# Sums of the last layer's weights by adding DMAs: begun at the first output projection in place of the first attention, at a shorter interval

## The chip, the core and the metric

The kernel runs on one core of a Trainium2 chip. The metric is the device time of one execution in microseconds, the median of several runs. Five engines work beside each other, each through its own instructions in a fixed order: PE (TensorE, matrix products), ACT (ScalarE), DVE (VectorE), POOL (GpSimd) and SP (SyncE, which here only issues DMAs). ACT and POOL issue DMAs too, as instructions among their others.

## The reference

A two-layer encoder over 512 tokens (a grid of 8 x 64) of width 1024, in float32:

```python
for layer in range(2):
    hn = rmsnorm(h, norm_mix[layer])
    if layer == 0:   # 8 heads of grouped-query attention and 8 of latent attention, one output projection
        h = h + hybrid_attention(hn, ...)
    else:            # 16 heads, each query sees a clamped 8 x 16 window, learned bias
        h = h + neighbourhood_attention(hn, ...)
    h = h + sq_relu_mlp(rmsnorm(h, norm_ffn[layer]), ffn_w_up[layer], ffn_w_down[layer])
return rmsnorm(h, final_norm)

def sq_relu_mlp(h, w_up, w_down):
    u = jax.nn.relu(h @ w_up)
    return (u * u) @ w_down      # 1024 -> 4096 -> 1024
```

## The kernel before

Everything lies feature by token: `hT` holds the residual as 8 tiles of 128 features x 512 tokens. For float32 accuracy each operand is split into a high part (ACT rounds it, `whi`) and a low part (DVE or POOL subtracts, `wlo`), and a product is three matmuls, high x high, high x low and low x high (lines 515 to 517). Weights come by DMA from the SP queue into `raw` or a slot `a`, ACT and DVE split them (lines 212 and 202), PE uses them; the loads run up to five chunks ahead.

Most of the two MLPs uses seven products in place of eight (Strassen's scheme). The weights of such a product are sums of blocks. In `seven_chunk` POOL makes the sums in three instructions (lines 302 to 304) out of a loaded chunk, then ACT (line 308) and DVE (line 309) split the result, then PE runs 21 matmuls of 256 columns (lines 388 to 390).

The down product of the last layer's MLP is done in another way, in three sweeps over 11 pairs of row blocks. Its sums are made ahead, in DRAM, by `SumsAhead`: for each of the 11 pairs, ACT issues two copies of 512 KB from the weight tensor into a DRAM buffer `made` (line 810), and POOL issues four DMAs of 256 KB that add one half of a row block to another (line 804): two that add from the weight tensor and, one and two pairs later, two that add `made` to `made`. That is 22 copies and 44 additions. They are pinned to their places in the program (`keep_in_program_order`); who reads the sums is the sweep near the end (line 1304).

What paces them is a beat. `tick(us)` is called with each three matmuls and each quarter of an attention head, with a nominal time; whenever `every` nominal microseconds have gone by, one step of the generator `steps()` is taken, which issues one copy or one addition. `drain()` ahead of the sweeps takes what is left.

The stages in the order of the program: the first input projection; the first attention (`attend`: 16 heads of 4 query blocks, with the second part of the input projection, the latent projections and a part of the output projection filled in between the heads' matmuls); the rest of the output projection; the first MLP (`mlp(0)`: products with 6, 8 and 8 hidden blocks of plain or seven-fold form, then 10 more); the second attention (`attend_C`, whose order on PE, ACT, DVE and POOL is written out by hand); its output projection; the last MLP. Outside the second attention a scheduler orders each engine's instructions by its own estimates, so instructions near an added or removed one can change places.

In an attention head of the first kind PE makes scores (line 1039), DVE takes the row minimum (line 1043, in place of a maximum because the sign is turned) and a reciprocal (line 1046), ACT the exponential (line 1045), POOL the division (line 1047); PE transposes (line 1014), ACT and DVE split (lines 1016 and 1017), PE multiplies with the values (line 1027). Queries of the second to fourth pair of heads get their rotary positions in `rope_q` and `sum_q`: eight small DMAs from SP swap partitions (line 572), POOL multiplies (lines 576 and 577), DVE adds (line 645), ACT and DVE split (lines 647 and 648), and three more DMAs from SP place the parts (lines 649 to 651).

Of the kernel before, what the change touches and what calls it, by code (L numbers as in the profile page):

```python
# [30 lines left out]
def f32(ap):  # L31
    return ap.bitcast(F32)
# [3 lines left out]
def encoder_kernel(ctx: ExitStack, tc: tile.TileContext, ins, out, dbg=None):  # L36
# [24 lines left out]
    def nm(s):  # L61
        cnt[0] += 1
        return f"{s}_{cnt[0]}"
# [18 lines left out]
    def sbk():  # L82
        return bank("s", 2)

    def stb():
        return bank("t", 2)

    def ob():
        return bank("o", 1)
# [4 lines left out]
    def tiny(n, dt=F32):  # L94
        return tp.tile([P, n], dt, tag=f"ti{n}", name=nm("ti"))
# [369 lines left out]
    def tiles(c0, n):  # L465
        return [(c0 + o, min(P, n - o)) for o in range(0, n, P)]
# [5 lines left out]
    class Fill:  # L472
# [8 lines left out]
        def step(self):  # L481
            try:
                self.credit -= next(self.q[0][1])
            except StopIteration:
                self.q.pop(0)
# [15 lines left out]
    beat = dict(left=0.0, every=1.0, work=iter(()))  # L501

    def tick(us):
        beat["left"] -= us
        if beat["left"] <= 0:
            beat["left"] += beat["every"]
            next(beat["work"], None)
# [285 lines left out]
    class SumsAhead:  # L793
# [11 lines left out]

        def steps(self):
            for kp in range(self.n + 3):
                if kp < self.n:
                    for z in range(2):
                        tc.keep_in_program_order(ACT.dma_start(self.made[kp, z], self.w[kp, z]))  # L810
                        yield
                for back, to, src, of in ((1, (1, 1), (0, 1), self.w), (1, (0, 1), (0, 0), self.w),
                                          (2, (0, 0), (1, 1), None), (3, (1, 0), (0, 0), None)):
                    if 0 <= kp - back < self.n:
                        self.add(kp - back, to, src, of)
                        yield
# [166 lines left out]
    def fold(o, e):  # L983

        if e == 0:
            hold["pair"] = scratch()
        a, c, pair = 64 * e, scratch(), hold["pair"]
        ACT.activation(c[0:64, :], o[64:128, :], AF.Copy)

        def add():  # L990
            DVE.tensor_tensor(pair[a : a + 64, :], o[0:64, :], c[0:64, :], op=ALU.add)
            if e:
                O.append(Slot())
                soon_a(lambda o=O[-1]: split(pair, o.pair()))

        soon(add)
# [6 lines left out]
    def attend(heads, step):  # L1003


        late_t, late_v = [], []

        def transpose(h, i, p):
            if i % 2 == 0:
                h["pt"] = Slot(), Slot()  # L1010
            h3, l3 = (s_.t.rearrange("p (k q) -> p k q", k=4)[:, :, (i % 2) * P : (i % 2 + 1) * P] for s_ in h["pt"])
            tb = stb()
            for k in range(4):
                PE.transpose(tb[:, k * P : (k + 1) * P], p[:, k * P : (k + 1) * P], ident)
            t3 = tb.rearrange("p (k q) -> p k q", k=4)
            ACT.activation(h3, t3, AF.Copy)
            DVE.tensor_tensor(l3, t3, f32(h3), op=ALU.subtract)
            if i % 2:
                late_v.append((h, i // 2, h["pt"]))

        def values(h, half, pt):
            if half == 0:
                h["o"] = ob()
            o = h["o"]
            for k in range(4):
                for n, m in enumerate(pt):
                    PE.matmul(o[:, 256 * half : 256 * half + 256], h["vlhs"](k), m.t[:, 256 * k : 256 * k + 256],
                              start=k == 0 and n == 0, stop=k == 3 and n == 1, skip_group_check=True)
            for s_ in pt:
                s_.free()  # L1030
            if half:
                fold(o, h["e"])
                h["after"]()

        def scores(h, i):
            s = sbk()
            pl = h["passes"](i)
            for n, (lh, rh) in enumerate(pl):
                PE.matmul(s, lh, rh, start=n == 0, stop=n == len(pl) - 1)  # L1039
            h["done"](i)  # L1040
            t = tiny(4)
            p = pp.tile([P, 512], F32, tag="p", name=nm("p"))
            DVE.tensor_tensor_reduce(p, s, zeros.to_broadcast([P, S]), op0=ALU.add, op1=ALU.min, scale=h["scale"](i),
                                     scalar=3e38, accum_out=t[:, 1:2])
            ACT.activation(p, p, AF.Exp, bias=t[:, 1:2], scale=-1.0, accum_out=t[:, 2:3])
            DVE.reciprocal(t[:, 3:4], t[:, 2:3])  # L1046
            POOL.tensor_scalar(p, p, t[:, 3:4], 1.0, op0=ALU.mult, op1=ALU.mult)  # L1047
            return p

        for h in heads:  # L1050
            for i in range(4):
                ripe = list(late_v)
                tick(1.3)
                p = scores(h, i)
                if len(late_t) == 3:
                    transpose(*late_t.pop(0))
                late_t.append((h, i, p))
                if ripe:
                    values(*late_v.pop(0))
                step(h, i)  # L1060
        for x in late_t:
            transpose(*x)
            while late_v:
                values(*late_v.pop(0))
            fill.run(1.5)

    def heads_A():
        for h in range(8):
            t, e, kv = h // 2, h % 2, h // 4
            if e == 0 and t < 3:  # L1070
                rope_q(t + 1)
            q, k = QA[t].pair(), KA[kv].pair()

            def done(i, t=t, e=e):
                if e == 1 and t < 3 and i == 0:
                    sum_q(t + 1)
                if i == 3 and e:
                    QA[t].free()
                    if t % 2:
                        KA[t // 2].free()  # L1080

            yield dict(e=e, done=done, scale=lambda i, h=h: hold["scA"][:, i, h : h + 1],
                       passes=lambda i, q=q, k=k, e=e: [(q[:, e, i * P : (i + 1) * P], k[:, z, :]) for z in range(2)],
                       vlhs=lambda kt, kv=kv: VAv[:, kt, kv, :], after=VA.free if h == 7 else lambda: None)

    def heads_B(g):
        fill.until(f"v{g}")
        Q, K, V = (QKV[g][z] for z in "QKV")
        vv = [s_.t.rearrange("p (i h e) -> p i h e", i=2, h=4) for s_ in V]
        for j in range(4):  # L1090
            q, k = Q[j].pair(), K[j].pair()

            def passes(i, q=q, k=k):
                ts = slice(i * P, (i + 1) * P)
                return [(q[0:96, 0, ts], k[0:96, 0, :]), (q[0:96, 1, ts], k[0:96, 0, :]),
                        (q[0:96, 0, ts], k[0:96, 1, :])]

            def done(i, j=j):
                if i == 3:
                    Q[j].free()  # L1100
                    K[j].free()

            def after(j=j):
                if j == 3:
                    for s_ in V:
                        s_.free()

            yield dict(e=j % 2, done=done, after=after, scale=lambda i: hold["scB"][:, i : i + 1], passes=passes,
                       vlhs=lambda kt, j=j: vv[kt // 2][:, kt % 2, j, :])
# [3 lines left out]
    def all_heads():  # L1113
        yield from heads_A()
        yield from heads_B(0)
        yield from heads_B(1)
# [14 lines left out]
        fill.run(1.5)  # L1131

    ahead1 = SumsAhead(ins["ffn_w_down"][1], FIRST, RAW // 2)
    beat.update(every=11.0, work=ahead1.steps())
    fill.add("z", product(w_in, 0, XP, tiles(768, 384), ev_cq, three))
    fill.add("z", product(w_in, 0, XP, tiles(1152, 256), ev_ckv, three, eng=POOL))
    fill.add("z", rotary_key())
    fill.add("z", latents())
    projB(0, False)
    attend(all_heads(), step)  # L1140
    fill.until("out")
    ok = [s_.pair() for s_ in O[4:]]
    flip[0] = 1
# [178 lines left out]
    class Sweeps:  # L1322
# [66 lines left out]
        def run(self, R):  # L1389
# [33 lines left out]
            starts = {(0, 0), (0, 1), (1, 0), (2, 1)}  # L1423
            tail, held, waiting = [], {}, []
            for i, (kind, kp) in enumerate(steps):
                if i + 1 < len(steps):
                    ready_[steps[i + 1]] = self.tokens(*steps[i + 1])
# [583 lines left out]
```

## Time and profile before

| what | value |
|---|---|
| median of 3 runs | 1180.82 us (1178.72 to 1182.04) |
| the profiled execution | 1178.83 us |
| its span, from first to last instruction | 1176.9 us |
| granted clock of TensorE | 0.998 of full |
| PE busy | 1150.5 us, 98% of the span |
| DVE, ACT, POOL busy | 902.3 us, 655.6 us, 514.1 us |
| first copy, last addition | at 66.63 us, at 865.79 us |

The profiled execution is 1.93 us longer than its span, and 1.99 us shorter than the median. Issuing a DMA is not counted as busy time on ACT and SP; on POOL the additions appear as instructions of some 0.8 us. In rows of the timeline the columns are start, duration, engine and line (a q behind the engine's name is its sequencer, which issues DMAs), operation, tiles, and in brackets how long the engine had been idle and what ended that.

### The profile page before, as it was taken

How to read it: one execution, taken by the hardware profiler on the slowest of the kernel's cores; microseconds unless marked ns; L12 is line 12 of the kernel's file. 1: busy time of each engine (PE TensorE's matmuls, PEld its weight loads, DVE VectorE, ACT ScalarE, POOL GpSimd, SP SyncE). 2: the span in 40 equal slices, each digit the busy share in tenths (PEclk: the TensorE clock that was granted, in tenths of full speed). 3: DMA queues.
4: the chain of work that ended last, by engine and by line, in shares of the span. 5: the costliest groups of instructions: out<-in, count | busy, mean ns of one | idle time of the engine just before them, and what ended most of it. 6: DMA issues, size and time to landing. Idle time of an engine off the chain costs nothing.

```text
span 1176.9 us, 20495 instructions
## 1 busy us (share of the span) xinstructions
PE 1150.5 (98%) x7380; PEld 1024.7 (87%) x7380; DVE 902.3 (77%) x1565; ACT 655.6 (56%) x1116; POOL 514.1 (44%) x658
## 2 busy tenths in 40 slices
PE   9988999999999999999999999999999999999997
PEld 8657778888889899998998989988888999999995
DVE  4788998888977458878795676666898887699855
ACT  5467676664526246672463555555562666676625
POOL 3267444223682376828911333332179998300000
PEclk9999999999999999999999999999999999999999
DMA  7234344433645853435536775655345323375802
GB/s 245 66 94 127 87 126 106 137 79 110 184 130 134 257 177 98 135 101 163 160 72 163 185 172 150 167 146 147 119 109 161 90 82 91 99 250 172 268 1 72
DMA packets 120117, 159.78 MB, mean 136 GB/s; under 512 B 10884, under 2 KB 84529, under 8 KB 119665
## 3 DMA queue, kind: packets, MB, share of 16 engines
q1 hardware_dynamic: 109920, 127.95, 36.0%
q0 software_dynamic: 8640, 17.85, 8.9%
q10 hardware_dynamic: 1456, 12.69, 3.4%
q8 instruction: 58, 0.95, 0.3%
q14 instruction: 43, 0.34, 0.1%
HBM read 136.03 MB, written 29.36 MB: 141 GB/s over the span
## 4 chain that ended last, share of the span: by engine, by line
PE 82%; DVE 4%; ACT 1%; issue 1%; POOL 0%; DVEq 0%; ACTq 0%; POOLq 0%
PE mm L515 7%; PE mm L516 7%; PE mm L517 7%; PE mm L390 3%; PE mm L389 3%; PE mm L388 3%; PE t L389 2%; PE t L388 2%; PE t L390 2%; PE s L516 2%; PE s L517 2%; PE s L515 2%; PE s L390 2%; PE s L388 2%; PE s L389 2%; PE s L1039 1%
## 5 line engine op out<-in xcount | busy, mean ns | idle before, releaser
L309 DVE TENSOR_TENSOR wlo<-a,whi 128x896 fp32r<-128x896 f32 x116 | 149.3, 1291 | 63.0 <-ACT whi L308 62.4
L308 ACT ACTIVATE whi<-a 128x896 fp32r<-128x896 f32 x116 | 109.8, 949 | 127.1 <-PE o L516 41.3
L515 PE MATMUL mm<-a,whi 128*128 128x512 f32 x443 | 178.7, 405 | 0.6 <-DVE a L957 0.4
L517 PE MATMUL mm<-a,wlo 128*128 128x512 f32 x443 | 174.5, 395 | 0.4 <-DVE wlo L202 0.3
L516 PE MATMUL mm<-a,whi 128*128 128x512 f32 x443 | 174.6, 394 | 0.0
L202 DVE TENSOR_TENSOR wlo<-raw,whi 128x1024 fp32r<-128x1024 f32 (+4 forms) x103 | 122.7, 1195 | 48.3 <-ACT whi L212 45.9
L212 ACT ACTIVATE whi<-raw 128x1024 fp32r<-128x1024 f32 (+3 forms) x106 | 101.4, 959 | 86.8 <-PE s L516 29.4
L302 POOL TENSOR_TENSOR a<-a 128x128 f32<-128x128 f32 x116 | 76.8, 665 | 98.4 <-DMA a<-in_ffn_w_up_dram 73.0
L304 POOL TENSOR_TENSOR a<-a 128x128 f32<-128x128 f32 x116 | 106.7, 922 | 8.9
L303 POOL TENSOR_TENSOR a<-a 128x256 f32<-128x256 f32 x116 | 97.4, 843 | 8.9
L517 PEld LDWEIGHTS mm<-a,wlo 128*128 128x128 f32 x443 | 83.1, 188 | 19.5 <-DVE wlo L202 1.1
L515 PEld LDWEIGHTS mm<-a,whi 128*128 128x128 f32 x443 | 83.3, 188 | 18.1 <-DVE hT L973 0.6
L516 PEld LDWEIGHTS mm<-a,whi 128*128 128x128 f32 x443 | 83.5, 188 | 15.1
L390 PE MATMUL mm<-a,wlo 128*128 128x256 f32 x330 | 92.7, 281 | 0.0
L389 PE MATMUL mm<-a,whi 128*128 128x256 f32 x330 | 92.6, 281 | 0.0
L388 PE MATMUL mm<-a,whi 128*128 128x256 f32 x330 | 92.5, 280 | 0.0
L1047 POOL TENSOR_SCALAR p<-p,ti 128x512 f32<-128x512 f32 x64 | 46.9, 735 | 88.0 <-DVE ti L1046 68.9
L1709 POOL TENSOR_SCALAR p<-p,ti 128x256 f32<-128x256 f32 x64 | 35.5, 566 | 97.8 <-DVE ti L1708 85.6
L389 PE MATMUL t<-a,whi 128*128 128x256 f32 x232 | 65.2, 281 | 0.0
L388 PE MATMUL t<-a,whi 128*128 128x256 f32 x232 | 65.1, 281 | 0.0
L390 PE MATMUL t<-a,wlo 128*128 128x256 f32 x232 | 65.0, 280 | 0.0
L390 PEld LDWEIGHTS mm<-a,wlo 128*128 128x128 f32 x330 | 62.1, 188 | 0.3 <-DVE wlo L309 0.2
(403 smaller groups left out, 3566.1 us busy)
## 6 DMA issues: line engine op xcount, KB each, us to landing
a<-in_ffn_w_up_dram SPq DMA_DIRECT2D x101, 256.0 KB
raw<-in_ffn_w_down_dram SPq DMA_DIRECT2D x32, 512.0 KB
made<-in_ffn_w_down_dram ACTq DMA_DIRECT2D x22, 512.0 KB
a<-made SPq DMA_DIRECT2D x38, 256.0 KB
raw<-in_od_w_qkv_dram SPq DMA_DIRECT2D x64, 128.0 KB
a<-in_ffn_w_down_dram SPq DMA_DIRECT2D x29, 256.0 KB
raw<-in_ffn_w_up_dram SPq DMA_DIRECT2D x12, 512.0 KB
raw<-in_ffn_w_down_dram SPq DMA_DIRECT2D x24, 256.0 KB
```

Of the source, the lines that this page charges most:

```text
L202: z = lambda: (eng or DVE).tensor_tensor(to, src, f32(high), op=ALU.subtract)
L212: ACT.activation(hi[:, 0:m], raw[:, 0:m], AF.Copy)
L303: POOL.tensor_tensor(r[:, 4:6], r[:, 2:3].to_broadcast([P, 2, P]), r[:, 0:7:6], op=ALU.add)
L304: POOL.tensor_tensor(r[:, 7], r[:, 3], r[:, 5], op=ALU.subtract)
L308: ACT.activation(hi[:, 0:896], raw[:, 128:1024], AF.Copy)
L309: DVE.tensor_tensor(lo[:, 0:896], raw[:, 128:1024], f32(hi[:, 0:896]), op=ALU.subtract)
L388: PE.matmul(o, wh, x[:, 0], start=kp == 0 and n in (0, 1, 3, 5), stop=False, skip_group_check=True)
L389: PE.matmul(o, wh, x[:, 1], start=False, stop=False, skip_group_check=True)
L390: PE.matmul(o, wl, x[:, 0], start=False, stop=kp == self.np - 1, skip_group_check=True)
L515: PE.matmul(o, wh, xh, start=first, stop=False)
L516: PE.matmul(o, wh, xl, start=False, stop=False)
L517: PE.matmul(o, wl, xh, start=False, stop=last)
```

## The change

The beat is no longer started ahead of the first attention but after it, where the rest of the output projection begins, and it is taken every 6 nominal us, not every 11. Near the end of the generator, where no copy is left, one beat is left empty ahead of each of the last two groups of additions.

```diff
         def steps(self):
             for kp in range(self.n + 3):
+                if kp > self.n:
+                    yield
                 if kp < self.n:
                     for z in range(2):
                         tc.keep_in_program_order(ACT.dma_start(self.made[kp, z], self.w[kp, z]))
...
     ahead1 = SumsAhead(ins["ffn_w_down"][1], FIRST, RAW // 2)
-    beat.update(every=11.0, work=ahead1.steps())
     fill.add("z", product(w_in, 0, XP, tiles(768, 384), ev_cq, three))
...
     projB(0, False)
     attend(all_heads(), step)
+    beat.update(every=6.0, work=ahead1.steps())
     fill.until("out")
```

The copies and additions are the same in number and size. In the order of POOL, 9 of the 44 additions stood in the first attention, 20 in the first MLP, 12 in the second attention and 3 in the last MLP; now none stands in the first attention, 39 ahead of the second and 5 in it. Of ACT's 22 copies 8 stood in the first attention, 10 in the first MLP and 4 in the second attention; now 2 stand at the end of the first attention and 20 in the first MLP. Lines from 808 on are now numbered 2 higher.

DVE in the first attention, at the third pair's rotary sum (line 645 before and now; `a_988` and `a_985` are the low parts of a transposed block of weights of attention, `sc_881` and `sc_879` the rotated query). Before:

```order
L991 TENSOR_TENSOR sc_861<-o_931,sc_1004 64x512
L645 TENSOR_TENSOR sc_881<-sc_881,sc_872 128x512
L1046 RECIPROCAL ti_1043<-ti_1043 128x1
L1017 TENSOR_TENSOR a_988<-t_1049,a_987 128x4x128
L872 TENSOR_TENSOR a_1007<-sc_861,a_1007 128x512
L648 TENSOR_TENSOR sc_1037<-sc_881,a_871 128x512
```

Now, on the same engine and at the same place:

```order
L993 TENSOR_TENSOR sc_859<-o_928,sc_1001 64x512
L1045 ISA p_1040,ti_1039<-s_1029,zeros,scA 128x512
L1045 ISA ti_1039 128x1
L1019 TENSOR_TENSOR a_985<-t_1045,a_984 128x4x128
L874 TENSOR_TENSOR a_1004<-sc_859,a_1004 128x512
L645 TENSOR_TENSOR sc_879<-sc_879,sc_870 128x512
L1048 RECIPROCAL ti_1039<-ti_1039 128x1
L1045 ISA p_1068,ti_1067<-s_1064,zeros,scA 128x512
L1045 ISA ti_1067 128x1
L648 TENSOR_TENSOR sc_1033<-sc_879,a_869 128x512
```

The subtraction on the transposed block, for which PE's product with the values waits, stood behind the rotary sum and now stands ahead of it; the low part of the rotated query (line 648) has another row minimum ahead of it.

ACT, at the fourth copy of before, in the same stretch of the first attention (`sc_1004` is a part of a head's output). Before:

```order
L1016 ACTIVATE a_922<-t_960 128x4x128
L1016 ACTIVATE a_987<-t_989 128x4x128
L521 ACTIVATE a_1012<-mm_647,gT 128x512
L810 DMA made_621<-in_ffn_w_down_dram 16x8192
L988 ACTIVATE sc_1004<-o_931 64x512
L1045 ACTIVATE p_1044,ti_1043<-p_1044,ti_1043 128x512
```

Now:

```order
L1018 ACTIVATE a_984<-t_986 128x4x128
L1047 ACTIVATE p_979,ti_978<-p_979,ti_978 128x512
L990 ACTIVATE sc_1001<-o_928 64x512
L1018 ACTIVATE a_984<-t_1045 128x4x128
L212 ACTIVATE whi_1057<-raw_799 128x512
```

The copy is gone from here, and the second part of the transposed block is taken ahead of the next exponential.

POOL in the second group of seven-fold products of the first MLP (the 46th to 48th chunk; each chunk is one tile `a`). Before:

```order
L302 TENSOR_TENSOR a_5352<-a_5352 128x128
L303 TENSOR_TENSOR a_5352<-a_5352 128x256
L304 TENSOR_TENSOR a_5352<-a_5352 128x128
L302 TENSOR_TENSOR a_5382<-a_5382 128x128
L303 TENSOR_TENSOR a_5382<-a_5382 128x256
L304 TENSOR_TENSOR a_5382<-a_5382 128x128
L302 TENSOR_TENSOR a_5413<-a_5413 128x128
L303 TENSOR_TENSOR a_5413<-a_5413 128x256
L304 TENSOR_TENSOR a_5413<-a_5413 128x128
```

Now:

```order
L304 TENSOR_TENSOR a_5356<-a_5356 128x128
L804 DMA made_621<-made_621 128x512
L302 TENSOR_TENSOR a_5387<-a_5387 128x128
L303 TENSOR_TENSOR a_5387<-a_5387 128x256
L304 TENSOR_TENSOR a_5387<-a_5387 128x128
L302 TENSOR_TENSOR a_5417<-a_5417 128x128
L303 TENSOR_TENSOR a_5417<-a_5417 128x256
L304 TENSOR_TENSOR a_5417<-a_5417 128x128
L804 DMA made_621<-made_621 128x512
```

Two additions have come between chunks where none stood. From the 28th to the 52nd chunk POOL has 7 additions now and had 4.

## Prediction

> **What bounds the kernel now.** I read the page's span and the chain first, then PE's waits, then busy time by stage.
>
> ```profile
> span 1176.9 us, 20495 instructions
> PE 82%; DVE 4%; ACT 1%; issue 1%; POOL 0%; DVEq 0%; ACTq 0%; POOLq 0%
> core 0: us, PE busy (x) PEld busy (x) DVE busy (x) ACT busy (x) POOL busy (x), PEclk, DMA share, GB/s
> 60.00:200.00 140.00, 128.66 (x719) 101.49 (x718) 122.27 (x288) 98.03 (x210) 74.44 (x82) 1.00 0.40 105
> 260.00:620.00 360.00, 358.81 (x2335) 325.94 (x2334) 278.94 (x342) 181.48 (x243) 202.57 (x252) 1.00 0.51 141
> 620.00:840.00 220.00, 219.35 (x1287) 191.04 (x1287) 147.14 (x375) 120.50 (x269) 64.42 (x111) 1.00 0.62 157
> 840.00:1140.00 300.00, 300.00 (x2283) 288.20 (x2282) 249.89 (x336) 168.99 (x234) 138.99 (x168) 1.00 0.45 137
> ```
>
> PE sets the time: it is idle 1.2 us in the first MLP (260 to 620), 0.7 us in the second attention and its surroundings (620 to 840) and never from there to 1140. Only the first attention has something to give: from 60 to 200 us PE idles 140 - 128.66 = 11.3 us. So the change can gain some 11 us at the very most, and it moves its work into a stage where only a loss can arise. Whatever PE gains at 60 to 200 us reaches the end, since PE is the bound afterwards.
>
> What PE waits for, over the whole span:
>
> ```profile
> PE o L1027 <- DVE a L1017: 4.6, 6, 1.7
> PE s L1039 <- DVE ti L1043: 2.3, 1, 2.3
> PE s L1039 <- DVE a L638: 1.4, 1, 1.4
> PE s L1039 <- DMA a<-sc: 1.2, 2, 0.7
> PE t L1731 <- POOL p L1709: 0.2, 1, 0.2
> ```
>
> DVE's chain of softmax ends most of the waits, and small DMAs of the rotated queries end 1.2 us of them. The two waits of 2.3 and 1.4 us are at the start of the first head, before anything but the first copy has been issued.
>
> **Taking the copies out of the first attention.** Eight of the 22 copies and 9 of the 44 additions leave it.
>
> ```profile
> L810 ACTq DMA_DIRECT2D made<-in_ffn_w_down_dram x22: 496/496/618, 66.6 to 732.8; - x22
> L804 POOL DMA_DIRECT2D made<-made x22: 802/842/1419, 197.9 to 865.8; - x22
> q0 software_dynamic: 8640, 17.85, 8.9%
> q10 hardware_dynamic: 1456, 12.69, 3.4%
> 79.07 0.60 ACT L1016 ACTIVATE a<-t 128x512 fp32r<-128x512 f32 x1 [0.73 <-PE t L1014]
> 79.08 0.52 ACTq L810 DMA_DIRECT2D made<-in_ffn_w_down_dram  x1
> ```
>
> Issuing: eight copies by 0.50 us are 4 us of ACT's sequencer. The last two rows show one issued while an activation of 0.60 us runs, and the next activation needed the engine only later, so I take 0 (at most the whole 4 us, were none covered). Nine additions by 0.84 us are 7.6 us of POOL; in the list of PE's waits above no wait of the first attention is ended by POOL, so 0 directly.
>
> The transfers cost more. ACT's queue q10 moved 12.69 MB in 3.4% of the span on all 16 engines: 40 us, so a copy of 0.52 MB holds the 16 engines for 1.65 us. That meets the rotary DMAs:
>
> ```profile
> 90.37 6.41 SPq L572 DMA_DIRECT2D sc<-a  x8
> 95.33 0.52 ACTq L810 DMA_DIRECT2D made<-in_ffn_w_down_dram  x1
> 100.02 1.28 POOL L577 TENSOR_TENSOR sc<-sc,a 128x512 f32<-128x512 f32 x1 [3.22 <-DMA sc<-a]
> 101.34 1.76 DVE L645 TENSOR_TENSOR sc<-sc,sc 128x512 f32<-128x512 f32 x1 [1.11 <-POOL sc L577]
> 103.09 0.67 DVE L1017 TENSOR_TENSOR a<-t,a 128x512 fp32r<-128x512 f32 x1
> 103.81 1.09 PE L1027 MATMUL o<-a,a 128*128 128x256 f32 x7 [1.69 <-DVE a L1017]
> 104.50 0.68 DVE L648 TENSOR_TENSOR sc<-sc,a 128x512 fp32r<-128x512 f32 x1
> 106.54 0.46 SPq L651 DMA_DIRECT2D a<-sc  x1
> 110.52 0.73 PE L1039 MATMUL s<-a,a 128*128 128x512 f32 x2 [0.70 <-DMA a<-sc]
> 87.22 0.50 PE L1039 MATMUL s<-a,a 128*128 128x512 f32 x1 [0.51 <-DMA a<-sc]
> 119.28 1.27 POOL L577 TENSOR_TENSOR sc<-sc,a 128x512 f32<-128x512 f32 x1
> ```
>
> The eight small DMAs are issued until 96.78, with a copy put in at 95.33. POOL waits 3.22 us for them, DVE 1.11 us for POOL, the subtraction for the values stands behind DVE's rotary sum, and PE waits 1.69 us. The third rotary group, with no copy beside it, found its data landed (119.28, no wait). This is the clearest loss that the change takes away: the copy is gone, and the new order of DVE has that subtraction ahead of the rotary sum. The Trainium skill ("DMA: Bandwidth & Descriptors", section "Issuing engines are not separate DMA queues") says that DMAs of all issuing engines run on the same 16 DMA engines and interleave; by it the rotary DMAs lose up to the copy's 1.65 us, and if the queues were separate nothing would come back on that side. POOL's 3.22 us against no wait bear the first out.
>
> But the gain has a next waiter. Scores of the next pair need the low part (line 648) and its DMA, and PE waited 0.70 us for that at 110.52. In the new order two instructions on a row minimum stand between lines 645 and 648, and the sum itself comes later. DVE was free at 101.34 - 1.11 = 100.23. From there six instructions, at the 0.67 and 0.68 us that lines 1017 and 648 show, end line 648 at about 104.3, against 105.18 before. So the rotated query is 0.9 us earlier while PE arrives 1.69 us earlier: if nothing else fills PE, 0.8 us come back as a wait for scores. The term lies between -0.9 and -1.7 us if the copy is gone and nothing else moves, and at 0 if the reshuffle feeds DVE later; I take -0.9. The wait of 0.51 us at 87.22 has a copy (79.08) shortly ahead of its DMAs: between 0 and -0.5; half of it, -0.2.
>
> **The new order of the first attention.** PE, DVE and ACT change places in some hundred rows. Of the 11.3 us of idle time the rows above explain 1.69 + 0.70 + 0.51 = 2.9, the start of the first head 3.7; 4.7 us are left, spread over waits for DVE. A reshuffle can remove them or add as many: -4.7 to +4.7. Lighter ACT and POOL queues speak for the gaining side, yet I found no issue on the path, so I take -0.5.
>
> **The second attention.** It loses its 4 copies and 7 of its 12 additions. PE waited for POOL once, 0.2 us (line 1731 above). 0 to -0.6 (all 0.65 us of idle there); I take -0.1. At its start, two additions now stand between POOL's DMAs for the first keys and queries; there POOL had idled 41.5 us and then twice 1 us:
>
> ```profile
> 633.10 1.10 POOL L1617 DMA_DIRECT2D a<-a  x2 [41.50 <-DVE a L872]
> 635.20 0.52 POOL L1637 DMA_DIRECT2D a<-a  x1 [1.00 <-ACT a L1632]
> 644.57 0.71 PE L1705 MATMUL s<-a,a 128*128 128x256 f32 x4
> ```
>
> The first addition fits into the idle 1.00 us, the scores come 8 us later: 0, at most 0.8 us each, so +1.6.
>
> **The first MLP.** It gets what the other stages lose: 20 copies, before 10, and 39 additions, before 20. From the queue rows above, 17.85 MB in 8.9% of the span are 5.9 us a MB on all 16 engines, 1.5 us for an addition of 0.26 MB; 19 more of these and 10 copies by 1.65 us are 45 us over 360, which lifts the DMA share from 0.51 to some 0.64. POOL's order has 7 instead of 4 additions between the 28th and 52nd chunk, where POOL's lead over PE shrinks to its smallest:
>
> ```profile
> 430.00:512.00 82.00, 81.07 (x680) 80.37 (x679) 64.25 (x72) 52.53 (x66) 62.05 (x78) 1.00 0.42 111
> 581.05 0.81 POOL L804 DMA_DIRECT2D made<-in_ffn_w_down_dram  x1
> 581.62 0.76 POOL L302 TENSOR_TENSOR a<-a 128x128 f32<-128x128 f32 x1
> 503.81 1.37 POOL L302 TENSOR_TENSOR a<-a 128x128 f32<-128x128 f32 x1 [0.73 <-DMA a<-in_ffn_w_up_dram]
> 506.08 0.46 POOL L304 TENSOR_TENSOR a<-a 128x128 f32<-128x128 f32 x1
> 508.06 0.94 ACT L308 ACTIVATE whi<-a 128x896 fp32r<-128x896 f32 x1
> 509.03 1.09 DVE L309 TENSOR_TENSOR wlo<-a,whi 128x896 fp32r<-128x896 f32 x1 [0.49 <-ACT whi L308]
> 512.58 0.28 PE L388 MATMUL mm<-a,whi 128*128 128x256 f32 x1
> ```
>
> For the 52nd chunk POOL ends at 506.54, ACT starts at 508.06 (1.5 us of slack), DVE ends at 510.12 and PE comes at 512.58 (2.5 us more). An addition takes 0.57 us of POOL until the next instruction (581.05 to 581.62); three more are 1.7 us, of which idle POOL (62.05 of 82 us busy, and a wait for data at 503.81) absorbs most. Against 4.0 us of slack: 0. If each took the longest issue of the rows, 1.419 us, and all fell behind, 4.3 us against 4.0: +0.3. With more DMAs the loaded chunks land later, too; the DMA share is 0.42 there, so I take 0, and +1.5 as the end, the 1.65 us of a copy in front of one late load.
>
> **Sum.** -0.9 - 0.2 - 0.5 - 0.1 + 0 = -1.7 us on the profiled execution of 1178.83: 1177.1. The median of the runs lies 1.99 us above that execution, so I say 1179.1. A change of this kernel can be told from none from about 0.3%, 3.5 us; this one is below.
>
> **Rivals.**
> 1. *The first attention is freed for good* (faster, about 1174.6): the rotary chain gains its 1.7 and 0.5 us, nothing returns at the scores, and the reshuffle takes 4 of the other 4.7 us: -6.2. For it: all terms are on PE's path. Against: line 648 is later in DVE's order.
> 2. *The new order costs* (slower, about 1185.5): scores of a pair of heads wait for a rotated query that DVE now makes later. It decides as soon as line 648 falls more than the 1.7 us gained behind; two such waits of the size of the 2.3 us row make +4.7. For it: the two instructions now ahead of line 648, and two rotary groups in that state; against: the small DMAs land earlier.
> 3. *POOL falls behind in the first MLP* (slower, about 1185.4): additions that PE's stretch cannot hide. The Trainium skill ("SBUF — State Buffer", section "SBUF: two separate sides") tells of a trap in which DMAs issued from POOL stall while DVE holds a port that both share. As a mechanism of this kernel: were all 7 additions of that stretch held as long as the longest issue, 1.419 us, plus a subtraction of DVE of 1.09 us each, 7 by 2.51 less the 4 by 0.57 hidden now are 15.3 us; less 4.0 us of slack and a third of POOL's 82 - 62.05 = 20 us of idle time there, +4.6. Against it: the additions of that stretch took 0.81 us, as everywhere.
> 4. *Nothing comes of it* (1180.8): the waits of the first attention end on something else at the same time, since six waits for line 1017 make 4.6 us and only one of them has a copy in its chain.
>
> **Chances.** The forecast, -1.7 with its own range of -3.5 to +0.5: 0.35. Rival 1: 0.32, nearly all of it beyond 3.5 us. Rival 2: 0.16, rival 3: 0.06, both mostly beyond +3.5. Rival 4: 0.11. With the edges of the forecast's own range that makes faster by over 0.3% 0.36, within it 0.43, slower 0.21. For eight in ten I go from rival 1 with somewhat more (1173.0) to rival 2 with a little less (1184.5).
>
> **What the profile of the changed kernel would show.** Right: PE's idle time from 60 to 200 us falls from 11.3 to about 9.5; POOL's wait for the rotary data near 100 us (3.22) is below 1.5; the values' product no longer waits 1.69; a wait of PE for the rotated query grows; no copy before 200 us; idle time of PE in 260 to 620 stays at 1.2. Wrong: PE idle in the first MLP above 3 us behind ACT's line 308 (rival 3), or new waits of PE's scores of over 1.5 us in the first attention (rival 2), or idle there below 6 us (rival 1).

## Result, and the profile after

The changed kernel takes 1184.15 us (median of 9 runs, 1182.40 to 1184.72), the kernel before 1180.33 (9 runs, 1178.64 to 1182.46): ratio 1.0028, 95% interval 1.0018 to 1.0038. It is slower by 0.28%, 3.8 us; the forecast was 1.7 us faster. The two profiled executions differ by 5.5 us (spans 1176.9 and 1182.4), more than the medians, since that of before is at the low end of its runs.

Busy time by stage after the change (columns as before: stretch, its length, busy PE, weight load, DVE, ACT, POOL, granted clock, DMA share, GB/s):

```profile
core 0: us, PE busy (x) PEld busy (x) DVE busy (x) ACT busy (x) POOL busy (x), PEclk, DMA share, GB/s
60.00:200.00 140.00, 132.25 (x748) 106.80 (x749) 123.60 (x296) 101.33 (x216) 71.47 (x77) 0.99 0.30 78
260.00:620.00 360.00, 354.37 (x2285) 319.75 (x2283) 270.73 (x327) 174.79 (x234) 215.09 (x269) 1.00 0.62 165
430.00:520.00 90.00, 85.08 (x681) 81.70 (x680) 66.77 (x76) 55.05 (x74) 68.03 (x88) 1.00 0.52 125
620.00:840.00 220.00, 217.97 (x1295) 190.50 (x1296) 145.58 (x377) 116.93 (x263) 58.69 (x104) 1.00 0.51 138
```

PE's idle time falls from 11.3 to 7.75 us in the first attention (second column, 140.00 less 132.25), rises from 1.2 to 5.6 us in the first MLP and from 0.65 to 2.0 us around the second attention. Most of the first MLP's loss lies between 430 and 520 us (PE idles 4.9 us there). The DMA share of the first MLP rose from 0.51 to 0.62, close to the 0.64 worked out ahead.

What PE waits for in the changed kernel, from 60 to 200 us (the first two lines), from 420 to 520 (two) and from 620 to 700 us (one); line numbers from 808 on are two higher than before:

```profile
PE s L1041 <- DVE ti L1045: 2.9, 2, 2.4
PE o L1029 <- DVE a L1019: 1.3, 3, 0.6
...
PE s L390 <- DVE wlo L309: 2.4, 4, 0.7
PE mm L390 <- DVE wlo L309: 2.3, 5, 0.7
...
PE s L1707 <- DMA a<-sc: 1.3, 1, 1.3
```

The softmax's wait (line 1017 before, 1019 after) fell from 4.6 to 1.3 us. In the first MLP, between 420 and 520 us, PE waits nine times for DVE's low parts of the weights, where it waited once, 0.9 us, before. The last line is a new wait of 1.3 us, for a small move of the queries at the start of the second attention.

Followed by stages, PE reaches the end of the first attention 3.7 us earlier than before and the 17th of the seven-product chunks still 3.7 us earlier; the 52nd it reaches 3.4 us later. So 7.1 us go between these two:

```profile
423.75 0.28 PE L388 MATMUL mm<-a,whi 128*128 128x256 f32 x1
...
420.04 0.28 PE L388 MATMUL mm<-a,whi 128*128 128x256 f32 x1
516.00 0.28 PE L388 MATMUL mm<-a,whi 128*128 128x256 f32 x1
```

The first row is the 17th chunk before (the 52nd, at 512.58, stands in the prediction): 88.83 us for these 35 chunks. The other two are after: 95.96 us. This time is the measure in all that follows.

The chain there starts at POOL. In POOL's program order the differences of the 22nd and 23rd chunk come behind those of four and five later chunks. POOL before, then the conversion of the 23rd chunk on ACT:

```profile
418.56 0.47 POOL L302 TENSOR_TENSOR a<-a 128x128 f32<-128x128 f32 x1 [1.62 <-DMA a<-in_ffn_w_up_dram]
427.11 0.81 POOL L804 DMA_DIRECT2D made<-in_ffn_w_down_dram  x1
427.68 1.26 POOL L302 TENSOR_TENSOR a<-a 128x128 f32<-128x128 f32 x1
429.84 0.46 POOL L304 TENSOR_TENSOR a<-a 128x128 f32<-128x128 f32 x1
433.83 0.96 ACT L308 ACTIVATE whi<-a 128x896 fp32r<-128x896 f32 x1 [1.26 <-POOL a L304]
```

The same rows after, with DVE and PE behind them:

```profile
420.81 0.46 POOL L302 TENSOR_TENSOR a<-a 128x128 f32<-128x128 f32 x1 [1.54 <-DMA a<-in_ffn_w_up_dram]
425.81 0.80 POOL L804 DMA_DIRECT2D made<-in_ffn_w_down_dram  x1
431.44 0.81 POOL L804 DMA_DIRECT2D made<-in_ffn_w_down_dram  x1
433.62 0.46 POOL L304 TENSOR_TENSOR a<-a 128x128 f32<-128x128 f32 x1
434.12 1.79 ACT L308 ACTIVATE whi<-a 128x896 fp32r<-128x896 f32 x2 [3.87 <-POOL a L304]
435.10 1.16 DVE L309 TENSOR_TENSOR wlo<-a,whi 128x896 fp32r<-128x896 f32 x1 [2.54 <-ACT whi L308]
436.32 0.39 PE L390 MATMUL s<-a,wlo 128*128 128x256 f32 x1 [0.69 <-DVE wlo L309]
```

Before, the 23rd chunk's last difference ends at 430.30, 3.5 us ahead of ACT. (The wait of 1.26 us that the profile puts down to POOL in ACT's row is not for this chunk: the difference of line 304 that ended just then, at 433.74, is that of a later one.) Afterwards it ends at 434.08 and ACT starts 0.04 us later, having idled 3.87 us. Three things add up. PE is 3.7 us earlier. The weights that POOL waits for land 2.3 us later (its start behind the load moves from 418.56 to 420.81). From there to the end POOL takes 13.3 us instead of 11.7, with two additions in it, not one; an addition takes 0.57 us of this, the rest is POOL's own differences, which take longer when they meet DVE (see rival 3 below). ACT and DVE are then just in time for each further chunk, and one more delay shows at PE each time.

The tightest places are further on. Before the change, POOL's last difference of the 37th and of the 41st chunk, each with ACT's conversion of the same chunk, and then ACT's two conversions after the change:

```profile
470.31 1.19 POOL L304 TENSOR_TENSOR a<-a 128x128 f32<-128x128 f32 x1
471.88 0.94 ACT L308 ACTIVATE whi<-a 128x896 fp32r<-128x896 f32 x1
481.74 1.19 POOL L304 TENSOR_TENSOR a<-a 128x128 f32<-128x128 f32 x1
483.30 1.78 ACT L308 ACTIVATE whi<-a 128x896 fp32r<-128x896 f32 x2
...
473.02 0.95 ACT L308 ACTIVATE whi<-a 128x896 fp32r<-128x896 f32 x1 [5.42 <-POOL a L304]
485.60 0.95 ACT L308 ACTIVATE whi<-a 128x896 fp32r<-128x896 f32 x1 [5.75 <-POOL a L304]
```

Before, POOL was 0.4 us ahead at both, and ACT came to them without idling; now ACT idles 5.42 and 5.75 us for them.

### The profile page after: what moved, and what is told of

Same layout as the page of the kernel before. It is cut to its first block, busy times and chain, and to the rows that moved or that the text cites. A ratio compares the mean times of both kernels' runs of the same rounds, so it can differ in the third digit from the quotient of the medians.

```text
span 1182.4 us, 20489 instructions
## 1 busy us (share of the span) xinstructions
PE 1154.6 (98%) x7380; PEld 1027.1 (87%) x7380; DVE 895.3 (76%) x1565; ACT 655.2 (55%) x1116; POOL 516.6 (44%) x658
## 4 chain that ended last, share of the span: by engine, by line
PE 76%; DVE 5%; POOL 2%; issue 2%; ACT 2%; DMA 2%; DVEq 0%; POOLq 0%; ACTq 0%
PE mm L515 7%; PE mm L517 7%; PE mm L516 7%; PE mm L390 3%; PE mm L389 3%; PE mm L388 3%; PE s L516 2%; PE s L517 2%; PE s L515 2%; PE t L388 2%; PE t L389 2%; PE t L390 2%; PE s L390 2%; PE s L389 1%; PE s L388 1%
## 5 line engine op out<-in xcount | busy, mean ns | idle before, releaser
L309 DVE TENSOR_TENSOR wlo<-a,whi 128x896 fp32r<-128x896 f32 x116 | 142.6, 1232 | 74.6 <-ACT whi L308 73.9
L302 POOL TENSOR_TENSOR a<-a 128x128 f32<-128x128 f32 x116 | 77.2, 668 | 96.1 <-DMA a<-in_ffn_w_up_dram 65.5
L303 POOL TENSOR_TENSOR a<-a 128x256 f32<-128x256 f32 x116 | 113.3, 979 | 8.8
L304 POOL TENSOR_TENSOR a<-a 128x128 f32<-128x128 f32 x116 | 93.1, 803 | 8.9
```

The lines of the kernel that those rows point to most:

```text
L303: POOL.tensor_tensor(r[:, 4:6], r[:, 2:3].to_broadcast([P, 2, P]), r[:, 0:7:6], op=ALU.add)
L304: POOL.tensor_tensor(r[:, 7], r[:, 3], r[:, 5], op=ALU.subtract)
L309: DVE.tensor_tensor(lo[:, 0:896], raw[:, 128:1024], f32(hi[:, 0:896]), op=ALU.subtract)
```

## Experiments

All are timed against the kernel before on the same chip (its medians in the three sessions were 1180.04, 1180.17 and 1180.45). The last column is the measure above, from the profiles: 88.83 us before, 95.96 after. It comes from one profile each; the kernels with one pause and with two pauses differ only behind the end of the first MLP and show 90.9 and 91.9 us, so a difference of about 1 us is not told apart.

| kernel | median us | ratio, 95% interval | PE idle 260-620 us | 17th to 52nd chunk, us |
|---|---|---|---|---|
| later start, interval 11.0 | 1179.76 | 0.9996 [0.9987, 1.0005] | 4.2 | 92.8 |
| old start, interval 6.0 | 1190.20 | 1.0089 [1.0075, 1.0103] | 5.75 | 96.6 |
| pause in the second product | 1179.14 | 0.9990 [0.9979, 1.0001] | 3.1 | 90.9 |
| narrow additions | 1179.00 | 0.9991 [0.9982, 1.0001] | 4.1 | 91.8 |
| two pauses | 1175.37 | 0.9967 [0.9955, 0.9979] | 3.8 | 91.9 |
| bias rows on ACT | 1185.17 | 1.0049 [1.0035, 1.0062] | 7.0 | 96.2 |
| pause elsewhere | 1181.38 | 1.0016 [1.0007, 1.0024] | 4.95 | 95.6 |
| interval 9.0, two pauses | 1177.55 | 0.9979 [0.9970, 0.9987] | 3.05 | 91.3 |
| long pause | 1172.04 | 0.9938 [0.9925, 0.9950] | 0.76 | 88.0 |
| old start, interval 11.0, two pauses | 1179.38 | 0.9995 [0.9985, 1.0004] | 1.8 | 89.3 |
| copies only | 1175.78 | 0.9956 [0.9942, 0.9970] | 2.1 | 89.9 |
| no empty beats | 1182.08 | 1.0014 [1.0005, 1.0023] | 6.6 | 96.65 |

**The two parts apart.** `every=11.0` in the changed kernel:

> The later start with the old interval of 11.0. Theory 1 (traffic: at the shorter interval, copies and additions between 330 and 435 us delay the loads of the weights of the second seven-product stretch, POOL forms their differences late, and PE waits between 434 and 499 us): the first attention keeps its 3.6 us, the first MLP loses nothing (PE idle 260 to 620 us at most 1.8 us), the start of the second attention costs less than 0.7 us, the rest of the sums goes beside the second MLP, where PE has no idle time: about 1176.7 us, 3 to 4 us less than before. Theory 2 (POOL's own time for the additions, whatever they move): the same here, 1176.7. Theory 3 (the order that a later start gives costs the first MLP, not the interval): the loss of 4 us in the first MLP stays, 1181 to 1184.

```profile
60.00:200.00 140.00, 132.24 (x762) 106.66 (x760) 124.85 (x298) 102.37 (x218) 72.51 (x79) 1.00 0.30 80
260.00:620.00 360.00, 355.77 (x2321) 323.00 (x2320) 269.60 (x339) 176.97 (x235) 202.96 (x252) 1.00 0.51 143
```

The first attention keeps its gain, but the first MLP still loses: a miss for all theories. There are as many sums as before around the stretch (DMA share 0.51 in both), and still 4.0 of the 4.9 us that PE was earlier at the 17th chunk are gone at the 52nd. So PE's earlier arrival is part of the cause: with sums in flight, what feeds it does not come as much earlier.

`every=6.0` at the old start:

> The old start, ahead of the first attention, with the interval of 6.0. Theory 1: in the first attention there are nearly twice as many copies and additions, so its PE idle grows from 11.3 us to 13 or more; in the first MLP the loss of about 4 us comes too, and the start of the second attention is free of sums (they end near 500 us): 1184 to 1189. Theory 2: the same, since POOL issues as many additions. Theory 3 (it is the late start that costs): the first MLP as before, 1180 to 1183.

As theory 1 and 2 had it, though slower than their range (and PE idles 12.35 us from 60 to 200, less than the 13 expected): the first attention ends 4.1 us later than before, and the 35 chunks of the first MLP take 7.8 us more. Not all of that is the sums': in this profile the granted clock is 0.5 for 3.4 us at 74, at 91 and at 446 us, the last of these within the chunks, where no other profile has such a dip. The interval is the harmful part; the later start is a gain that does not reach the end.

**When the sums run.** The work of the beat is set aside around the second product of the first MLP (`z == 1`):

```
+            if z == 1:
+                kept, beat["work"] = beat["work"], iter(())
             for c, gen in enumerate(gens):
 ...
+            if z == 1:
+                beat["work"] = kept
```

> As the changed kernel, but no copy and no addition is due during the second product of the first MLP (PE 376 to 420 us), where SP issues the rows of biases and the loads for the next stretch; they move behind. Theory 1: the loads land earlier and POOL is on time for the 22nd and 23rd chunk, so PE idle 260 to 620 us falls from 5.6 us to 2.5 or less: 1180 to 1181.5. Theory 2: the additions of 420 to 500 us are all still there, so 5 us stay: 1183.5 to 1185.

```profile
260.00:620.00 360.00, 356.86 (x2334) 324.58 (x2333) 269.67 (x343) 178.13 (x239) 214.78 (x263) 1.00 0.59 159
```

The median is 5.0 us less than that of the changed kernel, more than theory 1 expected, and PE's idle time is 3.1 us, not the 2.5 or less. The time of the 35 chunks falls by 5.1 of the 7.1 us, although the 17 sums from 420 to 512 us are all there. The control, `z == 2` in the same two places:

> A control: the same pause of the sums as in the first run with a pause, but in the third product of the first MLP (PE 516 to 560 us), behind the stretch that lost time. Theory 1: the loss of 430 to 520 us stays (PE idle 260 to 620 us 4.5 to 6 us), 1183 to 1185. If any pause helps, since it only takes sums out of the first MLP: about 1180.

```profile
260.00:620.00 360.00, 355.05 (x2293) 320.69 (x2292) 268.20 (x328) 176.63 (x237) 209.27 (x263) 1.00 0.59 158
```

With the same DMA share of 0.59 the stretch keeps its loss (95.6 us). It is the sums from 376 to 420 us, ahead of the stretch that loses, that matter most: six of them in the changed kernel, one with the first pause. (The median is 1.6 us below what was expected; the first scores of the second attention wait 0.6 us here, 1.3 us in the changed kernel.)

**Traffic or POOL's time.** First with `[:, 0:64]` on both sides of the addition, then with `add` returning at once:

> As the changed kernel, but each addition moves only the first 64 of its 512 columns (the sums of the others are left out): as many additions, each of 128 rows on POOL, with an eighth of their traffic; the copies are whole. Theory 1: PE idle 260 to 620 us falls from 5.6 us to 3 or less, 1180 to 1182 (more if the copies' traffic does most of it). Theory 2: POOL issues as often and as long, 5 us stay: 1183.5 to 1185.

> The changed kernel without its 44 additions (the sums are not formed, the copies are all there). If the additions' traffic and their time on POOL delay the 22nd and 23rd chunk, PE idle 260 to 620 us is 2 to 3.5 us instead of 5.6, and the start of the second attention waits for nothing: 1177 to 1178.5. If the copies (512 KB each, on ACT's queue) are the larger part, 4.5 us or more stay: 1180 to 1182.

```profile
260.00:620.00 360.00, 355.89 (x2306) 322.03 (x2305) 272.82 (x330) 177.05 (x236) 218.92 (x269) 1.00 0.48 142
...
260.00:620.00 360.00, 357.89 (x2337) 325.20 (x2337) 271.53 (x345) 177.56 (x237) 190.18 (x232) 1.00 0.45 140
```

The first row is that of the narrow additions: as many issues on POOL (269 instructions, as in the changed kernel) at a DMA share of 0.48. The second has no additions. By the 35 chunks, 4.2 of the 7.1 us are the additions' traffic (95.96 to 91.76), 1.9 us their issues with the eighth that is left (to 89.87), 1.0 us the copies and the earlier PE; the last two are near what one profile can tell apart. Theory 1 holds for most, theory 2 for a quarter at most. PE's idle time with narrow additions, 4.1 us, stayed above the 3 us of theory 1, and both medians are below the ranges that were expected.

**SP's queue.** Two of three writes of bias rows are issued by ACT:

```
-            SP.dma_start(bxv[0, c].rearrange("r h k -> r h k"), ...)
+            ACT.dma_start(bxv[0, c].rearrange("r h k -> r h k"), ...)
-            SP.dma_start(bxv[1, c][:, :, 128 - 128 * v : 256 - 128 * v], Fe.t[:, 256:384])
+            ACT.dma_start(bxv[1, c][:, :, 128 - 128 * v : 256 - 128 * v], Fe.t[:, 256:384])
```

> As the changed kernel, with all its sums at the interval of 6.0, but 32 of the 48 writes of bias rows are issued by ACT instead of SP. Theory 1 in its sharper form (the loads are late because they stand in SP's queue behind the rows, each held up while the DMA engines are full): the load of the 22nd chunk is issued several us earlier than 417 us, and PE idle 260 to 620 us falls from 5.6 us to 3 or less: 1180.5 to 1182. If it is the DMA engines alone, whatever queue, or ACT's 32 issues of 0.6 us delay its own conversions: 1183.5 to 1187.

The time is in the range of the second case. The load of the 23rd chunk is issued at 417.45 us, in the changed kernel at 417.39; PE now reaches the 17th chunk only 3.6 us earlier than before, having lost 2.3 us on the way, and the loss in the stretch is the same (96.2 us). But this does not clear SP's queue. SP's waits from 376 to 420 us in the changed kernel (two rows), with the first pause and with the rows on ACT:

```profile
SPq L300 <- DMA raw<-in_ffn_w_down_dram: 4.9, 4, 2.2
SPq L300 <- DMA a<-in_ffn_w_up_dram: 2.1, 2, 1.8
...
SPq L300 <- DVE wlo L309: 6.1, 2, 4.6
...
SPq L190 <- DMA bx<-a: 20.8, 6, 5.0
```

With the rows on ACT, SP still waits 20.8 us for rows to land, ahead of its loads of line 190, so the run took the issuing off SP and not the waiting. The first two rows show what delays the loads of the chunks (line 300) in the changed kernel: SP holds them back, 4.9 and 2.1 us, until earlier loads have landed (1.2 us of this before the change). With the pause it waits for DVE to be done with earlier chunks instead (6.1 us). The Trainium skill ("DMA: Bandwidth & Descriptors", section "Issuing engines are not separate DMA queues") says that DMAs of all issuing engines run on the same 16 DMA engines. That moving the rows to ACT brought no gain agrees with it; what within these engines makes a load land late was not measured.

**The start of the second attention.** A second pause, from the end of the first MLP to the end of the lead-in:

```
     mlp(0)
+    kept, beat["work"] = beat["work"], iter(())
 ...
     fill.run(LEAD)
+    beat["work"] = kept
```

> As the changed kernel with the pause of the second product, and a second pause: no copy or addition is due from the end of the first MLP until the second attention's lead-in is done. If sums in flight there delay the small moves of keys and queries (256 KB, 128 KB), for which PE waited 2.1 us at 641 us with one pause alone, that wait goes: PE idle 620 to 700 us falls to 0.3 us or less, 1176.5 to 1177.5. If the wait belongs to PE's earlier arrival and not to the sums, it stays: 1179.

In the changed kernel, POOL's moves of keys and queries with two additions among them, SP's last move of the queries, and PE's first scores:

```profile
637.48 1.10 POOL L1619 DMA_DIRECT2D a<-a  x2 [39.47 <-DVE a L874]
638.56 0.90 POOL L804 DMA_DIRECT2D made<-made  x1
639.59 0.55 POOL L1639 DMA_DIRECT2D a<-a  x1
640.91 0.52 POOL L1640 DMA_DIRECT2D a<-sc  x1 [0.77 <-DVE sc L1638]
641.42 0.91 POOL L804 DMA_DIRECT2D made<-made  x1
645.98 0.50 SPq L1644 DMA_DIRECT2D a<-sc  x1
650.23 0.47 PE L1707 MATMUL s<-a,a 128*128 128x256 f32 x2 [1.28 <-DMA a<-sc]
```

PE waits for SP's move (line 1644). It overwrites what POOL's move of line 1639 reads, so it comes after that one: 6.39 us after its issue here, 5.18 us before the change (635.20 and 640.38), 4.24 with narrow additions and 3.74 with two pauses. With two pauses:

```profile
620.00:700.00 80.00, 80.00 (x457) 69.53 (x456) 47.94 (x125) 40.07 (x89) 23.82 (x43) 1.00 0.70 175
```

PE has no idle time left there. It has none either with narrow additions, which POOL issues at the same places, so it is their traffic, not their place in POOL's queue. At 1175.37 us, 1.1 us below the range expected, this kernel is faster than before by 0.33%.

**Versions that keep more.** An interval of 9.0 with both pauses, and an interval of 6.0 whose first pause begins ahead of `stage` for `z == 1` and ends behind `stage` for `z == 2`, so that it covers both seven-product stretches:

> The later start with an interval of 9.0 and both pauses. Theory 1: the 3.7 us of the first attention are kept, the first MLP loses at most 2 us, the start of the second attention nothing, and the last sums fall into the second MLP, where PE has no idle time: 1175.5 to 1177.5, faster than both kernels. If the sums' end, then after 900 us, holds up POOL's chunks of the second MLP: 1179 or more.

> As the kernel with two pauses at the interval of 6.0, but the first pause lasts from the first seven-product stretch to the end of the second (PE 335 to 512 us), so that no sum runs beside it. If the 2 to 4 us that every kernel with the freed first attention still lost between its 17th and 52nd chunk come from sums, they go: at most 1 us, 1173 to 1174.5. If they are that stretch's own (the loads of the 37th and 41st chunk, which PE reaches earlier now), 2 to 3 us stay: 1175 to 1176.5.

The first came out at the upper end, 1177.55 us; its first MLP lost 2.5 us between the two chunks, not 2 at most. The second is the fastest of all, 1172.04 us, 0.62% below the kernel before and better than expected. Its stage and its 17th and 52nd chunk:

```profile
260.00:620.00 360.00, 359.24 (x2346) 326.62 (x2345) 277.92 (x346) 180.25 (x241) 203.26 (x247) 1.00 0.47 139
...
418.14 0.28 PE L388 MATMUL mm<-a,whi 128*128 128x256 f32 x1
...
506.14 0.28 PE L388 MATMUL mm<-a,whi 128*128 128x256 f32 x1
```

88.0 us for the 35 chunks, less than before the change, with PE there 5.6 us earlier. Between 318 and 498 us no copy or addition is issued in this kernel. So the early arrival costs nothing when no sums are in flight, and the 2 to 4 us that the other versions still lost were the sums'.

**Two checks of the rest.** The pauses alone in the kernel before, and the changed kernel without `if kp > self.n: yield`:

> The kernel before (start at the first attention, interval 11.0) with the two pauses alone. Its first attention has the sums still, its first MLP lost 1.2 us and the start of its second attention nothing. So 1179 to 1180.5; if the pauses were worth as much without the later start as with it, 1175 to 1177.

> The changed kernel without its two empty beats ahead of the last two groups: the last additions come 6 to 12 us earlier in the second attention. Every theory: no change against the changed kernel, 1183.5 to 1185.

The pauses alone are worth little (0.9995), the later start alone as little (0.9996), both with the interval of 6.0 make 0.9967: the start gives time that the pauses keep. Without the empty beats the profile has the same span (1182.3 us, from one of that kernel's longest executions) and the same loss in the stretch. Its median is 2.1 us lower than the changed kernel's, and below the range expected; the two intervals, 1.0005 to 1.0023 and 1.0018 to 1.0038, overlap, so this stays open.

## Why the prediction was wrong

- *The first attention: -0.9 - 0.2 - 0.5.* Right in sign, too small: PE's idle time fell by 3.6 us instead of 1.6. The waits of 1.69, 0.70 and 0.51 us are all gone, POOL no longer waits 3.22 us for the rotary data (its multiplication of line 577 starts at 97.99 without a wait), and the 0.8 us that a wait for the rotated query was to take back did not come: no wait for a DMA is left in that stage. No run tells the missing copies from the new order of instructions here, so which of the two gave the 3.6 us stays open. Rival 2 did not come either.
- *The first MLP: 0, at most +1.5.* This is the step that failed: 7.1 us between the 17th and the 52nd chunk. The slack of 4.0 us was read at the 52nd chunk, taking it for the tightest. POOL forms chunks in another order than ACT takes them. Matched by chunk, POOL's lead over ACT before was 3.5 us at the 23rd and 0.4 us at the 37th and 41st chunk, and 0.9 of the 1.2 us of idle time already there was one wait, at the 38th. It also priced the loads' later landing, at 0 with 1.5 us as the end, by the DMA share of 0.42 from 430 to 512 us. The loads of the 17th to 23rd chunk are issued earlier, from 371 to 417 us, where the share was already 0.67 before (343.7 to 423.7 us) and 0.74 after (340 to 420 us), and SP waits there for earlier loads to land. And the gain of the first attention was not subtracted from the slack.
- *The start of the second attention: 0, at most +1.6.* The bound held, the value did not: 1.3 us. It was priced as room in POOL's queue; it was the landing of the small moves, one of which has to wait for another.
- *The second attention proper: -0.1.* Nothing to tell apart.
- *Rival 3*, POOL behind in the first MLP at 0.06, is what happened, with its sign that PE's idle time there goes above 3 us, but not by its mechanism. The additions between the chunks took 0.80 and 0.81 us, as before, and only those issued right behind another took longer (up to 1.73 us, once the 52nd chunk was done). No issue between the chunks was held up the way that the Trainium skill's rule on the shared port ("SBUF — State Buffer", section "SBUF: two separate sides") tells for DMAs issued from POOL. POOL was late since its input landed late, and by one more ordinary addition. What DVE does hold up there is POOL's own differences of 128 columns (lines 302 and 304). In the kernel before, from 395 to 515 us, 27 of them took 0.72 to 1.37 us and began while DVE ran line 309, and each of the 27 ended 0.31 to 0.33 us after DVE's; the short ones took some 0.46 us. That was there all along and did not grow: the differences of the 36 chunks take POOL 83.6 us before and 82.3 after.

In sum on the profiles: -3.7 in the first attention, +7.1 in the second seven-product stretch, +0.9 around the first products of the second attention (near 619 us), +1.3 at the first scores of the second attention: +5.6 against +5.5 of span.

## What to carry to other kernels

Slack must be read for each buffer by name, from producer to consumer, and not by position in two engines' lists: the tightest place may be a chunk that one engine makes out of order. A gain ahead of a stretch comes off the slack of that stretch, unless its loads start earlier too. Background transfers are placed best by which stretch has loads to spare, not by a constant beat: pausing them where weights are fetched just in time, and at the start of the second attention, turned 0.28% slower into 0.62% faster.

## What was not expected of the hardware

Behind the same wait of PE the granted clock fell to a half in some profiles and not in others. The changed kernel behind its wait of 2.38 us for DVE (the timeline, then the windows), and the kernel without empty beats behind the same wait:

```profile
74.33 0.99 PE L1041 MATMUL s<-a,a 128*128 128x512 f32 x2 [2.38 <-DVE ti L1045]
75.12 0.63 PE L516 MATMUL mm<-a,whi 128*128 128x512 f32 x1
...
74.30:77.70 3.40, 3.37 (x9) 2.63 (x10) 2.81 (x8) 2.60 (x7) 0.12 (x1) 0.55 0.00 0
...
75.27 0.73 PE L1039 MATMUL s<-a,a 128*128 128x512 f32 x2 [2.38 <-DVE ti L1043]
75.85 0.40 PE L516 MATMUL mm<-a,whi 128*128 128x512 f32 x1
```

In the first, a matmul takes 0.63 us instead of 0.40, and the granted clock is 0.55 for 3.4 us. The Trainium skill ("TensorE: Matmul & The Clock Gate", section "Part 1: The HAM clock gate") tells of a gate that halves the clock after an idle window of about 3.4 us of a free-running counter; a slow phase of 3.4 us agrees, though the wait here is shorter than the window. Among the kernels with the later start, the five profiles with this dip end the first attention 181.1 to 181.6 us after its first score, the six others with none 179.6 to 180.0: 1.5 us, as much as several terms of the sum. Against the 184.3 us before, which had no dip in its profile, the first attention gains some 3.0 us with it and 4.5 us without. A dip does not always cost that: the kernel with the old start and two pauses has one of 3.4 us at 103 us and ends after 184.4 us.
